# A hybrid decoder step on one Trainium2 core: activations, per-layer input, conv state and norm weights handed over with features as rows, and the first gate and up products taken by turns over the row blocks of x

## The chip, the cores and the metric

The kernel runs on one core of a Trainium2 chip (trn2). The metric is device time in microseconds (us) from launch to end. The engines are PE (TensorE: PE for matmuls, PEld for weight loads), DVE (VectorE), ACT (ScalarE), POOL (GpSimd) and SP (SyncE, which here only issues DMAs). The host arranges the inputs before the launch; what it does is not in the metric.

## The reference, cut to what matters

One layer, for 256 prompt rows and 8 x 4 = 32 sample rows together (288 rows, all float32):

```python
h = h + 0.5 * ((silu(rms(h) @ wg1) * (rms(h) @ wu1)) @ wd1)      # FFN 1: 2048 -> 5632 -> 2048
cb, cc, ch, q, k, v, fl = split(rms(h) @ w_in)                    # 6152 columns
h = h + [rms(cb * conv3(cc * ch)) | rms(forget_attention(q, k, v, fl, paged cache))] @ w_out
h = h + 0.5 * ((silu(rms(h) @ wg2) * (rms(h) @ wu2)) @ wd2)      # FFN 2
h = h + sigmoid(rms(h) @ w_ple_gate) * (p @ w_ple_proj)           # p: 256 features a row
y = rms(h)
```

`rms(x)` scales a row by the inverse root of its mean square and each feature by a norm weight (gain). The convolution carries two earlier rows of each sample sequence (`state_conv`); the sample attention reads 64 pages of cached keys and values by a page table.

## The kernel before, in words

Everything is kept with **features as rows**: `h` is one tile of 128 partitions x 16 blocks x 288 columns, where block k holds features 128k to 128k+127 (a row block, 128 x 288). A product with a weight matrix takes 256 output columns at a time (`pair`, L276 to L308): two banks of PSUM, over all 16 row blocks. float32 is done as float32r in two parts: a value is split in hi and lo, and each 128 x 128 piece of weight takes three matmuls of 288 columns (L298 hi·xh, L299 hi·xl, L300 lo·xh). These are called main matmuls below.

- **Weights** arrive by SP in tiles of 4 row blocks x 256 columns, 512 KB (`load_upto`, L237 to L253), in a ring of `RAW` = 8 buffers: the ninth load waits until the first tile is split. A tile is split in two halves of 2 row blocks (`split_upto`, L257): ACT writes `whi` (L265), DVE `wlo` (L266). There are `HALVES` = 5 buffers for them, so splits run at most five halves ahead of PE. A tile is a **chunk** of 24 main matmuls; a half is 12.
- **x** is made the same way (`split`, L209): ACT `xh` (L210), DVE `xl` (L211), both with the gain column `gT`. The scaling by the inverse root comes later: squares (L226, L229) are added up in `acc` on POOL (L230; the last ones on DVE), PE sums over partitions (L182, L183), DVE and ACT work out the inverse root (L184 to L190), PE spreads it (L206) and DVE copies it into `rs` (L207). `rs` is first used when gate products leave PSUM (`tg`, L358; then ACT `sg` L360, POOL `sr` L362, and `hd`, L367, for up products).
- **The opening**: x comes in as in the reference, rows as rows, in 8 pieces `xa` (128 x 2 x 256) and 8 `xb` (32 x 256). PE turns each row block by three transposes (L412 to L414, in `x_turn`), DVE copies it into `h` (L415), and then it is split and squared. `first` (L432) ties this to the four chunks of the first gate product: turns are placed one chunk ahead, squares behind. The first up product begins when the gate product is through.
- **Gains**: the first norm's are turned by PE at the start (L147), the other seven vectors at step 44 of a written-out list of steps (`later_loads`): 7 loads, 4 more small loads (`bf`, `wf`, `pidx`, `ptb`), then one turn 20 chunks later. From `ptb` DVE works out `idx` (L167), the rows of the paged cache.
- **Keys of the cache**: `k_turn` (from step 50 on) fetches page j + 2 by an indirect DMA of POOL (`kg`, L458) and turns page j on DVE (`kt`, L467), which is written back by four DMAs of POOL (`KD`, L469).
- **Conv state and per-layer input** are loaded as in the reference and turned by PE (L876, 8 transposes; L1078 to L1080, 6).

The order within an engine is not written out: a scheduler places the instructions when the program is built, and each engine then runs its own in that order. `keep_in_program_order` pins some.

Of the kernel before, what the change touches and what calls it, by code (L numbers as in the profile page):

```python
# [25 lines left out]
P = 128  # L26
D = 2048
# [22 lines left out]
TSTEP = 16  # L50

# [37 lines left out]
def build(nc, tc, ctx, A, O):  # L89
# [18 lines left out]
    spare = {"tags": ("kt", "mm"), "at": 0}  # L108
# [22 lines left out]
    def load_gains(names, at, eng):  # L131
        rows = sum(A[n].shape[0] for n in names) // P
        t = W["xs" if at == 0 else "f1"][0].tile([rows, P], F32, name=f"gn{at}", bufs=1)
        r = 0
        for name in names:
            n = A[name].shape[0] // P
            d = eng.dma_start(t[r:r + n, :], A[name].rearrange("(k p) -> k p", p=P))
            if eng is sy:
                tc.keep_in_program_order(d)
            G[name] = at + r  # L140
            r += n
        return t, at

    def turn_gains(t, at):
        b = ktbank()
        r = t.shape[0]
        pe.transpose(b[:, :r], t, ident[:r, :r])  # L147
        v.tensor_copy(gT[:, at:at + r], b[:, :r])
# [75 lines left out]
    def squares(k, work, last_on_v=2):  # L224
        if k == 0:
            s.activation(acc, h[:, k, :], AF.Square)  # L226
        else:
            sq = work.tile([P, NT], F32, name="sq", tag="sq", bufs=2)
            s.activation(sq, h[:, k, :], AF.Square)  # L229
            (v if k >= KT - last_on_v else g).tensor_tensor(acc, acc, sq, ALU.add)  # L230

# [3 lines left out]
    state = dict(loaded=0, split=0, used=0, halves_used=0, chunk=0)  # L235
# [40 lines left out]
    def pair(src, c0, kts, act, evac, k_of=lambda k: k, late=0, tag="mm"):  # L276
# [4 lines left out]
        for ci, ks in enumerate(chunks):  # L281
            it = weight(src, ks[0], len(ks), c0)

            def fn(ci=ci, ks=ks, it=it):
# [3 lines left out]
                split_upto(state["halves_used"] + HALVES)  # L288
# [54 lines left out]
    def ffn(wg, wu, wd, nextgain, work):  # L343
# [3 lines left out]
        for gi, grp in enumerate(groups):  # L347
            def start():
                H["hi"] = work().tile([P, 8, NT], F32R, name="hh", tag="hh", bufs=2)
                H["lo"] = work().tile([P, 8, NT], F32R, name="hl", tag="hl", bufs=2)  # L350
            do(start)
            for pi, pr in enumerate(grp):
# [19 lines left out]
                steps.extend(pair(wg, pr * 256, list(range(KT)), xact, gate, **(dict(late=2, tag="va") if pr == 0 else {})))  # L372
                steps.extend(pair(wu, pr * 256, list(range(KT)), xact, up))
# [25 lines left out]
    def x_load(c):  # L399
        xs = W["xs"][0]  # L400
        cs = slice(c * 256, c * 256 + 256)
        xa = xs.tile([P, 2, 256], F32, name="xa", tag="xa", bufs=8)
        xb = xs.tile([NS, 256], F32, name="xb", tag="xb", bufs=8)
        tc.keep_in_program_order(sy.dma_start(xa, A["x_prompt"][:, cs].rearrange("(j p) c -> p j c", p=P)))
        tc.keep_in_program_order(sy.dma_start(xb, A["x_sample"][:, cs]))
        return xa, xb

    def x_turn(k):
        xa, xb = xin[k // 2]
        w = slice(k % 2 * P, k % 2 * P + P)  # L410
        t = ktbank()
        pe.transpose(t[:, 0:P], xa[:, 0, w], ident)  # L412
        pe.transpose(t[:, P:2 * P], xa[:, 1, w], ident)
        pe.transpose(t[:, 2 * P:NT], xb[:, w], ident[:NS, :NS])  # L414
        v.tensor_copy(h[:, k, :], t[:, :NT])  # L415
        split(X["hi"][:, k, :], X["lo"][:, k, :], h[:, k, :], gain("norm_ffn1", k))
# [6 lines left out]
    opened("xs", "right")  # L423
# [4 lines left out]
    def turns(c):  # L428
        for k in range(4 * c, 4 * c + 4):
            x_turn(k)  # L430

    def first(i, c):  # L432
        run = steps[i][1]

        def fn():
            if c == 0:
                turns(0)
            if c < 3:
                defer(lambda: turns(c + 1), 1)
            if c == 3:  # L440
                spare["tags"] = ("kt",)
                x_squares(3)
                norm_scale(rs, acc, D, 1)
            run()
            if c < 3:
                x_squares(c)
        steps[i] = (steps[i][0], fn)

    for c in range(4):
        first(2 + c, c)  # L450
# [36 lines left out]
    a, b = CONST_COLS["ident"][1:]  # L487
    s.dma_start(C[:, a:b], A["consts"][:, a:b])
    g1 = load_gains(["norm_ffn1"], 0, s)
    for its, _ in steps[2:6]:  # L490
        items.extend(its)
    xin = []
# [378 lines left out]
    def state_in():  # L871
        t = W["fp"][0].tile([16, CB * P], F32, name="stn")
        g.dma_start(t, A["state_conv"])
        b = ktbank()
        for i in range(CB):
            pe.transpose(b[:, 16 * i:16 * i + 16], t[:, i * P:i * P + P], ident[:16, :16])  # L876
# [304 lines left out]
```

## Time and profile before

| | |
|---|---|
| time, 3 runs | median 2389.52 us (2389.41 to 2391.86) |
| the profiled execution's own time | 2396.56 us |
| its span, first to last instruction | 2394.7 us |
| mean granted TensorE clock | 0.995 |
| PE busy | 2365.7 us (99%) |
| DVE, ACT, POOL busy | 60%, 44%, 21% |
| HBM read, written | 469.19 MB, 38.63 MB (212 GB/s over the span) |

How to read the rows that follow: in a window, "34.94 (x196)" is busy time and number of instructions, then come the granted clock, the busy share of the 16 DMA engines and GB/s. In a timeline, a row has start, duration, engine, line, operation, what it writes and reads, and in brackets the idle time before it and what ended that. Matmuls overlap: a row's duration is longer than the distance to the next start, and the distance is what counts. In the waits, a row has the total in us, how many, and the longest.

### The profile page before, as it was taken

The numbers are of one execution on the slowest core, as the hardware profiler recorded it, in microseconds if no ns is written. First come the engines' busy times: TensorE is split into PE (matmuls) and PEld (weight loads), VectorE is DVE, ScalarE is ACT, GpSimd is POOL, SyncE is SP. The second block draws the span as 40 slices with busy tenths as digits, with TensorE's granted clock in tenths as the row PEclk, the third lists the DMA queues.
The fourth block names the chain that finished last, engine by engine and source line by source line (L and its number), as shares of the span: only waits on it lengthen the run. The fifth ranks groups of instructions, "written<-read, shape, count | busy, mean of one in ns | idle before, by whom it ended". The sixth has DMA issues, their size and how long they took to land.

```text
span 2394.7 us, 46026 instructions
## 1 busy us (share of the span) xinstructions
PE 2365.7 (99%) x17856; PEld 2294.7 (96%) x17856; DVE 1430.9 (60%) x2588; ACT 1055.6 (44%) x1858; POOL 498.6 (21%) x688
## 2 busy tenths in 40 slices
PE   8999999999999999999999999999999999999997
PEld 8999999999999999888878899999999999999997
DVE  6556666666655585455456675555555555555765
ACT  5434443444444453333234454444444444444654
POOL 2025354353400011112545310000000000000100
PEclk9999999999999999999999999999999999999998
DMA  7478889898865556987887654545555555555542
GB/s 224 151 247 290 292 281 329 274 310 283 285 227 167 165 166 191 317 306 253 276 292 266 233 167 150 177 153 180 163 165 167 164 163 168 165 161 167 160 158 81
DMA packets 410703, 510.84 MB, mean 213 GB/s; under 512 B 22236, under 2 KB 379316, under 8 KB 406356
## 3 DMA queue, kind: packets, MB, share of 16 engines
q1 hardware_dynamic: 376596, 401.43, 52.4%
q0 software_dynamic: 33664, 106.13, 12.9%
q8 instruction: 140, 2.29, 0.4%
q14 instruction: 79, 0.65, 0.1%
q10 hardware_dynamic: 224, 0.34, 0.1%
HBM read 469.19 MB, written 38.63 MB: 212 GB/s over the span
## 4 chain that ended last, share of the span: by engine, by line
PE 93%; DMA 4%; issue 1%; DVE 1%; POOL 1%; ACT 0%; SPq 0%; POOLq 0%; DVEq 0%; ACTq 0%
PE mm L298 29%; PE mm L300 29%; PE mm L299 28%; DMA page<-in_cache_v_dram,idx 1%; PE va L726 1%; PE va L783 1%; PE va L298 1%; PE va L300 1%; PE va L299 1%; DMA wraw<-in_w_in_dram 1%; DMA bk<-FP 0%; POOL page L250 0%; DMA kg<-in_cache_k_dram,idx 0%; DMA wraw<-in_w_out_dram 0%; DMA xa<-in_x_prompt_dram 0%
## 5 line engine op out<-in xcount | busy, mean ns | idle before, releaser
L266 DVE TENSOR_TENSOR wlo<-wraw,whi 128x512 fp32r<-128x512 f32 x1384 | 967.5, 704 | 737.1 <-ACT whi L265 690.6
L265 ACT ACTIVATE whi<-wraw 128x512 fp32r<-128x512 f32 x1384 | 864.5, 630 | 989.0 <-PE mm L299 915.0
L298 PE MATMUL mm<-xh,whi 128*128 128x288 f32 x3712 | 1109.0, 299 | 0.8 <-DVE tg L358 0.8
L300 PE MATMUL mm<-xh,wlo 128*128 128x288 f32 x3712 | 1093.1, 295 | 3.6 <-DVE wlo L266 3.6
L299 PE MATMUL mm<-xl,whi 128*128 128x288 f32 x3712 | 1096.5, 295 | 0.0
L298 PEld LDWEIGHTS mm<-xh,whi 128*128 128x128 f32 x3712 | 697.1, 188 | 23.3 <-ACT whi L265 14.5
L300 PEld LDWEIGHTS mm<-xh,wlo 128*128 128x128 f32 x3712 | 700.1, 189 | 4.2 <-DVE wlo L266 4.2
L299 PEld LDWEIGHTS mm<-xl,whi 128*128 128x128 f32 x3712 | 698.3, 188 | 0.1
L298 PE MATMUL mm<-hh,whi 128*128 128x288 f32 x1408 | 416.8, 296 | 0.0
L299 PE MATMUL mm<-hl,whi 128*128 128x288 f32 x1408 | 415.4, 295 | 0.0
L300 PE MATMUL mm<-hh,wlo 128*128 128x288 f32 x1408 | 414.0, 294 | 0.0
L362 POOL TENSOR_TENSOR sr<-sg,rs 128x288 f32<-128x288 f32 x88 | 72.8, 828 | 1126.8 <-ACT sg L360 1126.7
L300 PEld LDWEIGHTS mm<-hh,wlo 128*128 128x128 f32 x1408 | 265.1, 188 | 0.0
L299 PEld LDWEIGHTS mm<-hl,whi 128*128 128x128 f32 x1408 | 264.3, 188 | 0.0
L298 PEld LDWEIGHTS mm<-hh,whi 128*128 128x128 f32 x1408 | 263.8, 187 | 0.0
L469 POOL DMA_DIRECT2D KD<-kt x256 | 142.5, 562 | 80.6 <-DVE kt L467 60.6
L230 POOL TENSOR_TENSOR acc<-acc,sq 128x288 f32<-128x288 f32 x66 | 57.1, 865 | 267.1 <-ACT sq L229 222.7
L380 DVE SCALAR_TENSOR_TENSOR h<-mm,h 128x288 f32<-128x288 f32 x192 | 86.7, 453 | 21.3 <-PE mm L300 20.8
L467 DVE STREAM_TRANSPOSE kt<-kg 128x1024 f32<-128x1024 f32 x64 | 79.2, 1238 | 29.0 <-DMA kg<-in_cache_k_dram,idx 22.3
L458 POOL DMA_INDIRECT kg<-in_cache_k_dram,idx x64 | 71.6, 1118 | 74.5 <-DMA wraw<-in_w_ffn_gate_dram 55.5
L360 ACT ACTIVATE sg<-tg 128x288 f32<-128x288 f32 x88 | 39.1, 445 | 104.7 <-DVE tg L358 104.7
L369 ACT ACTIVATE hh<-hd 128x288 fp32r<-128x288 f32 x88 | 39.2, 445 | 96.3 <-DVE hd L367 96.3
(294 smaller groups left out, 1544.0 us busy)
## 6 DMA issues: line engine op xcount, KB each, us to landing
wraw<-in_w_ffn_gate_dram SPq DMA_DIRECT2D x176, 512.0 KB, 3.7
wraw<-in_w_ffn_up_dram SPq DMA_DIRECT2D x176, 512.0 KB, 3.6
wraw<-in_w_ffn_down_dram SPq DMA_DIRECT2D x160, 512.0 KB, 3.6
wraw<-in_w_in_dram SPq DMA_DIRECT2D x96, 512.0 KB, 4.9
KD<-kt POOLq DMA_DIRECT2D x256, 128.0 KB, 5.6
KT<-KD SPq DMA_DIRECT2D x32, 1024.0 KB, 7.3
wraw<-in_w_out_dram SPq DMA_DIRECT2D x32, 512.0 KB, 4.4
wraw<-in_w_ple_gate_dram SPq DMA_DIRECT2D x32, 512.0 KB, 3.6
```

The lines of the kernel that those rows point to most:

```text
L230: (v if k >= KT - last_on_v else g).tensor_tensor(acc, acc, sq, ALU.add)
L265: s.activation(hi, x, AF.Copy)
L266: v.tensor_tensor(lo, x, hi.bitcast(F32), ALU.subtract)
L298: pe.matmul(o, hi[:, j % 2, w], xh, start=f, stop=False)
L299: pe.matmul(o, hi[:, j % 2, w], xl, start=False, stop=False)
L300: pe.matmul(o, lo[:, j % 2, w], xh, start=False, stop=l)
L362: g.tensor_tensor(r, u, rs, ALU.mult)
L369: s.activation(H["hi"][:, k, :], t, AF.Copy)
L380: v.scalar_tensor_tensor(h[:, k, :], o, 0.5, h[:, k, :], ALU.mult, ALU.add)
L458: g.indirect_dma_start(out=KG[j], out_offset=None, in_=A["cache_k"], in_offset=bass.IndirectOffsetOnAxis(ap=idx[:, j:j + 1], axis=0))
L467: v.transpose(t, KG.pop(j).rearrange("p (h d c) -> p d h c", d=4, c=32))
L469: g.dma_start(KD[j // 2, :, j % 2, i].rearrange("(d c) n -> c d n", c=32), t[32 * i:32 * i + 32].rearrange("c d h r -> c d (h r)"))
```

## The change

The host hands over `x` (both groups in one array), `p` and the conv state with features as rows, already in the kernel's 128 x blocks x rows layout (`by_feature`), and all eight vectors of weights as one 128 x 120 array (`gains`). So the 48 transposes of x, the turns of gains (2), conv state (8) and p (6), their copies out of PSUM and their tiles are gone. x is loaded straight into `h` in five loads, `gT` in one on ACT's queue, `consts` in one behind the eighth weight tile.

The chunks of the first gate and the first up product now alternate: gate over row blocks 0 to 3, up over 0 to 3, gate over 4 to 7, and so on. Up uses two `kt` banks of PSUM beside gate's two `va` banks, and both leave PSUM later (`late` 5 and 4). Weight tiles are loaded in the same alternation. The 16 squares run behind chunks 4 to 7, pinned in order, 7 of the adds on POOL and 8 on DVE (before 13 and 2). The sum over partitions is deferred by two chunks after the eighth, its spread by one more. In the list of steps, one step less stands ahead of `later_loads` and of `k_turn` (`closed("xs")` is gone), so both now come one chunk later in the program.

```diff
-    def squares(k, work, last_on_v=2):
+    def squares(k, work, last_on_v=2, pin=False):
...
-                steps.extend(pair(wg, pr * 256, list(range(KT)), xact, gate, **(dict(late=2, tag="va") if pr == 0 else {})))
-                steps.extend(pair(wu, pr * 256, list(range(KT)), xact, up))
+                lead = firstg and pi == 0
+                gs = pair(wg, pr * 256, list(range(KT)), xact, gate, **(dict(late=5 if lead else 2, tag="va") if pr == 0 else {}))
+                us = pair(wu, pr * 256, list(range(KT)), xact, up, **(dict(late=4, tag="kt") if lead else {}))
+                steps.extend([x for gu in zip(gs, us) for x in gu] if lead else gs + us)
...
+    def x_load(a, b):
+        tc.keep_in_program_order(sy.dma_start(h[:, a:b, :], A["x"][:, a:b, :]))
+
+    def x_split(a, b):
+        for k in range(a, b):
+            split(X["hi"][:, k, :], X["lo"][:, k, :], h[:, k, :], gain("norm_ffn1", k))
 
     def x_squares(c):
         for k in range(4 * c, 4 * c + 4):
-            squares(k, W["xs"][0])
+            squares(k, W["f1"][0], 8, True)
...
+    def first(c):
+        run = steps[2 + c][1]
 
         def fn():
             if c == 0:
-                turns(0)
...
+                x_split(0, 2)
+                split_upto(1)
+                x_split(2, 4)
+                state["lead"] = HALVES - 1
+            if c == 1:
+                x_split(4, 8)
+                state["lead"] = HALVES
+            if c in (2, 4):
+                x_split(4 + 2 * c, 8 + 2 * c)
             run()
+            if c >= 4:
+                x_squares(c - 4)
+            if c == 7:
+                norm_scale(rs, acc, D, 2, 1)
...
     def later_loads():
-        t = load_gains(["norm_mix", "norm_ffn2", "norm_ple", "norm_final", "norm_conv_out", "norm_attn_out", "conv_w"], 16, sy)
         small_loads()
-        defer(lambda: turn_gains(*t), 20)
-
-    steps.insert(14, ([], lambda: closed("xs")))
...
+    s.dma_start(gT, A["gains"])
+    for its, _ in steps[2:10]:
         items.extend(its)
     for c in range(4):
-        xin.append(x_load(2 * c))
-        xin.append(x_load(2 * c + 1))
-        load_upto(c + 1)
+        x_load(4 * c, 4 * c + (2 if c == 0 else 4))
+        load_upto(2 * c + 1)
+        if c == 0:
+            x_load(2, 4)
+        load_upto(2 * c + 2)
     items.clear()
-    tc.keep_in_program_order(sy.dma_start(C[:, b:], A["consts"][:, b:]))
-    turn_gains(*g1)
+    tc.keep_in_program_order(sy.dma_start(C, A["consts"]))
...
+        g.dma_start(M["st"].rearrange("p i b t -> p i (b t)"), A["state"])
...
+        g.dma_start(pa, A["p"])
...
+            s.activation(E["hi"][:, k, :], pa[:, k, :], AF.Copy)
+            v.tensor_tensor(E["lo"][:, k, :], pa[:, k, :], E["hi"][:, k, :].bitcast(F32), ALU.subtract)
...
+def by_feature(a):
+
+    return np.ascontiguousarray(a.reshape(a.shape[0], -1, P).transpose(2, 1, 0))
```

The order of the instructions at three places follows. First ACT in the opening, from its first block of x on; before (`xh` is a split block of x, `whi` a split half of weights, `sq` and `acc` squares):

```order
L229 ACTIVATE sq<-h 128x288
L210 ACTIVATE xh<-h,gT 128x288 x3
L265 ACTIVATE whi<-wraw 128x512 x2
L226 ACTIVATE acc<-h 128x288
L210 ACTIVATE xh<-h,gT 128x288
L229 ACTIVATE sq<-h 128x288 x2
L210 ACTIVATE xh<-h,gT 128x288 x2
L265 ACTIVATE whi<-wraw 128x512 x2
```

and now:

```order
L200 ACTIVATE xh<-h,gT 128x288 x2
L257 ACTIVATE whi<-wraw 128x512 x2
L200 ACTIVATE xh<-h,gT 128x288 x2
L257 ACTIVATE whi<-wraw 128x512 x2
L200 ACTIVATE xh<-h,gT 128x288 x4
L257 ACTIVATE whi<-wraw 128x512 x4
L200 ACTIVATE xh<-h,gT 128x288 x4
L257 ACTIVATE whi<-wraw 128x512 x4
L200 ACTIVATE xh<-h,gT 128x288 x4
L257 ACTIVATE whi<-wraw 128x512
L216 ACTIVATE acc<-h 128x288
```

For every four blocks of x there are now four halves of weights where there were two, and no square stands ahead of the last block of x.

Second SP's queue at the later small loads, in the fourth pair of gate and up; before:

```order
L242 DMA wraw<-in_w_ffn_up_dram 128x4x256 x4
L137 DMA gn_1692<-in_norm_mix_dram 16x128
L137 DMA gn_1692<-in_norm_ffn_dram 16x128
L137 DMA gn_1692<-in_norm_ple_dram 16x128
L137 DMA gn_1692<-in_norm_final_dram 16x128
L137 DMA gn_1692<-in_norm_conv_out_dram 8x128
L137 DMA gn_1692<-in_norm_attn_out_dram 8x128
L137 DMA gn_1692<-in_conv_w_dram 24x128
L166 DMA bf<-in_b_f_dram 8x1
L166 DMA wf<-in_w_in_dram 128x16x8
L166 DMA pidx<-in_page_table_dram 64x1
L166 DMA ptb<-in_page_table_dram 128x64
```

and now:

```order
L234 DMA wraw<-in_w_ffn_up_dram 128x4x256 x4
L234 DMA wraw<-in_w_ffn_gate_dram 128x4x256
L156 DMA bf<-in_b_f_dram 8x1
L156 DMA wf<-in_w_in_dram 128x16x8
L156 DMA pidx<-in_page_table_dram 64x1
L156 DMA ptb<-in_page_table_dram 128x64
L234 DMA wraw<-in_w_ffn_gate_dram 128x4x256 x3
```

The seven loads of gains are gone, and the four small loads now stand behind the first gate tile of the fifth pair.

Third DVE behind them (`idx` from `ptb`; `kt` turns a page of keys, `tg` takes a gate product out of PSUM); before:

```order
L167 TENSOR_SCALAR idx<-ptb,consts 128x64
L266 TENSOR_TENSOR wlo<-wraw,whi 128x512 x3
L467 STREAM_TRANSPOSE kt<-kg 128x1024
L266 TENSOR_TENSOR wlo<-wraw,whi 128x512
L467 STREAM_TRANSPOSE kt<-kg 128x1024
L266 TENSOR_TENSOR wlo<-wraw,whi 128x512 x2
L467 STREAM_TRANSPOSE kt<-kg 128x1024
L358 TENSOR_TENSOR tg<-mm,rs 128x288
```

and now:

```order
L157 TENSOR_SCALAR idx<-ptb,consts 128x64
L258 TENSOR_TENSOR wlo<-wraw,whi 128x512 x2
L450 STREAM_TRANSPOSE kt<-kg 128x1024
L258 TENSOR_TENSOR wlo<-wraw,whi 128x512 x2
L450 STREAM_TRANSPOSE kt<-kg 128x1024 x2
L258 TENSOR_TENSOR wlo<-wraw,whi 128x512 x2
L352 TENSOR_TENSOR tg<-mm,rs 128x288 x2
```

`idx` stands behind as many splits as before, but the first page is turned one split earlier, and the third two splits ahead of the first `tg` instead of just ahead of it.

More of the change, by code (lines that the diff above doesn't have):

```diff
@@ L50 @@
 TSTEP = 16
+GAINS = ("norm_ffn1", "norm_mix", "norm_ffn2", "norm_ple", "norm_final", "norm_conv_out", "norm_attn_out", "conv_w")
+A_ROWS = dict(norm_ffn1=D, norm_mix=D, norm_ffn2=D, norm_ple=D, norm_final=D, norm_conv_out=CB * P, norm_attn_out=NH * P,
+              conv_w=3 * CB * P)
 CONST_COLS = {}
@@ L106, in mmbank @@
         return bank("mm", BANKS["mm"])
-    spare = {"tags": ("kt", "mm"), "at": 0}
+    spare = {"tags": ("kt",), "at": 0}
     def ktbank():
@@ L129, in build @@
     G = {}
[L131 to L148, printed above, removed]
+    at = 0
+    for name in GAINS:
+        G[name] = at
+        at += A_ROWS[name] // P
     def gain(name, k):
@@ L222, in make_x @@
         squares(k, work)
-    def squares(k, work, last_on_v=2):
+    def squares(k, work, last_on_v=2, pin=False):
         if k == 0:
-            s.activation(acc, h[:, k, :], AF.Square)
+            i = s.activation(acc, h[:, k, :], AF.Square)
         else:
             sq = work.tile([P, NT], F32, name="sq", tag="sq", bufs=2)
-            s.activation(sq, h[:, k, :], AF.Square)
+            i = s.activation(sq, h[:, k, :], AF.Square)
             (v if k >= KT - last_on_v else g).tensor_tensor(acc, acc, sq, ALU.add)
+        if pin:
+            tc.keep_in_program_order(i)
     steps = []
     items = []
-    state = dict(loaded=0, split=0, used=0, halves_used=0, chunk=0)
+    state = dict(loaded=0, split=0, used=0, halves_used=0, chunk=0, lead=HALVES)
     def load_upto(n):
@@ L287, in fn @@
                 last = ci == len(chunks) - 1
-                split_upto(state["halves_used"] + HALVES)
+                split_upto(state["halves_used"] + state["lead"])
                 state["chunk"] += 1
@@ L347, in ffn @@
         for gi, grp in enumerate(groups):
+            firstg = gi == 0 and nextgain == "norm_mix"
             def start():
@@ L426, in build @@
     do(lambda: closed("f1"))
[L428 to L433, printed above, removed]
+    def first(c):
+        run = steps[2 + c][1]
         def fn():
             if c == 0:
-                turns(0)
[L438 to L443, printed above, removed]
-            run()
[L445 to L450, printed above, removed]
+                x_split(0, 2)
[7 more added lines that the diff above has]
+                x_split(4 + 2 * c, 8 + 2 * c)
+            run()
+            if c >= 4:
+                x_squares(c - 4)
+            if c == 7:
+                norm_scale(rs, acc, D, 2, 1)
+        steps[2 + c] = (steps[2 + c][0], fn)
+    for c in range(8):
+        first(c)
     KD = drp.tile([DB * PAGES // 2, P, 2, 4, NH * 32], F32, name="KD")
@@ L871, in state_in @@
     def state_in():
[L872 to L876, printed above, removed]
         M["st"] = cst.tile([P, CB, DB, 2], F32, name="st")
-        v.tensor_copy(M["st"].rearrange("p i b t -> p (i b t)"), b[:, :CB * 16])
+        g.dma_start(M["st"].rearrange("p i b t -> p i (b t)"), A["state"])
     def conv_pair(i):
@@ L1068, in ple_start @@
         w = W["pl"][0]
-        pa = w.tile([P, 2, PLE], F32, name="pa")
-        pb = w.tile([NS, PLE], F32, name="pb")
-        g.dma_start(pa, A["p_prompt"].rearrange("(j p) c -> p j c", p=P))
-        g.dma_start(pb, A["p_sample"])
+        pa = w.tile([P, 2, NT], F32, name="pa")
+        g.dma_start(pa, A["p"])
         E["hi"] = w.tile([P, 2, NT], F32R, name="ph")
@@ L1171 @@
     host["consts"] = constants()
+    host["x"] = by_feature(np.concatenate([host.pop("x_prompt"), host.pop("x_sample")]))
+    host["p"] = by_feature(np.concatenate([host.pop("p_prompt"), host.pop("p_sample")]))
+    host["state"] = by_feature(host.pop("state_conv"))
+    host["gains"] = np.ascontiguousarray(np.concatenate([host.pop(n) for n in GAINS]).reshape(-1, P).T)
     for name, a in host.items():
```

30 lines of the change are left out of this document (removed).

## Prediction

> **What bounds the kernel now.** I read the page's busy times first:
>
> ```profile
> PE 2365.7 (99%) x17856; PEld 2294.7 (96%) x17856; DVE 1430.9 (60%) x2588; ACT 1055.6 (44%) x1858; POOL 498.6 (21%) x688
> ```
>
> PE is the bound, so the question is where PE does not do main matmuls at full pace. PE by stretches (busy time, instructions, granted clock, DMA share, GB/s) shows two such places:
>
> ```profile
> 0.00:41.00 41.00, 34.94 (x196) 1.00 0.80 251
> 41.00:140.00 99.00, 99.00 (x743) 1.00 0.51 160
> 140.00:165.00 25.00, 20.60 (x125) 0.80 0.76 246
> 165.00:300.00 135.00, 135.00 (x1015) 1.00 0.89 295
> ```
>
> The last row gives the full pace: 135 / 1015 = 0.133 us for one matmul. Of the 196 instructions before 41 us, 48 are turns of x, one turns gains and 12 belong to the inverse root (the next rows), which leaves 135 main matmuls, worth 135 x 0.133 = 18.0 us. By 41.0 us PE is thus **23.0 us behind**. Between 140 and 165 us there is room for 25 / 0.133 = 188 and 125 run: 63 x 0.133 = **8.4 us lost**. Both places are touched. The timeline of PE in the opening, and the work for the inverse root:
>
> ```profile
> 4.56 0.45 PE L412 MATMUL mm<-consts,xa 128*128 128x128 f32 x1 [4.56 <-DMA xa<-in_x_prompt_dram]
> 9.65 0.61 PE L298 MATMUL va<-xh,whi 128*128 128x288 f32 x1
> 20.29 0.52 PE L300 MATMUL va<-xh,wlo 128*128 128x288 f32 x1
> 20.65 0.30 PE L298 MATMUL va<-xh,whi 128*128 128x288 f32 x1
> 34.94 0.61 PE L182 MATMUL kt<-consts,acc 128*128 128x1 f32 x4
> 35.48 0.22 PE L183 MATMUL kt<-consts,acc 128*32 128x1 f32 x2
> 35.63 0.40 PE L300 MATMUL va<-xh,wlo 128*128 128x288 f32 x1
> 40.12 0.97 PE L206 MATMUL kt<-diag,consts 128*128 128x128 f32 x6
> 41.03 0.40 PE L298 MATMUL mm<-xh,whi 128*128 128x288 f32 x1
> ```
>
> The first main matmul starts at 9.65 us, and durations halve only after 20.3 us: until then the array runs at half pace, though the clock column says 1.00. The inverse root takes (35.63 - 34.94) + (41.03 - 40.12) = 1.6 us of PE, and stays.
>
> The second place, on SP, DVE and PE:
>
> ```profile
> 133.00 0.49 SPq L137 DMA_DIRECT2D gn<-in_norm_mix_dram  x1
> 139.21 0.58 SPq L166 DMA_DIRECT2D ptb<-in_page_table_dram  x1
> 139.90 6.89 SPq L242 DMA_DIRECT2D wraw<-in_w_ffn_gate_dram  x4
> 134.26 0.69 DVE L266 TENSOR_TENSOR wlo<-wraw,whi 128x512 fp32r<-128x512 f32 x1
> 144.33 0.26 DVE L167 TENSOR_SCALAR idx<-ptb,consts 128x64 int32<-128x64 int32 x1 [4.58 <-DMA ptb<-in_page_table_dram]
> 144.50 1.89 DVE L266 TENSOR_TENSOR wlo<-wraw,whi 128x512 fp32r<-128x512 f32 x3
> 152.90 1.25 DVE L467 STREAM_TRANSPOSE kt<-kg 128x1024 f32<-128x1024 f32 x1 [6.51 <-DMA kg<-in_cache_k_dram,idx]
> 151.26 0.29 PE L299 MATMUL mm<-xl,whi 128*128 128x288 f32 x1
> 154.78 0.61 PE L300 MATMUL mm<-xh,wlo 128*128 128x288 f32 x1 [3.22 <-DVE wlo L266]
> 159.09 0.61 PE L298 MATMUL mm<-xh,whi 128*128 128x288 f32 x1 [0.77 <-DVE tg L358]
> 163.57 0.44 PE L298 MATMUL mm<-xh,whi 128*128 128x288 f32 x1
> 163.81 0.35 PE L299 MATMUL mm<-xl,whi 128*128 128x288 f32 x1
> ```
>
> DVE stands still for the first page of keys, with splits queued behind it; PE runs dry, and restarts with matmuls 0.24 us apart (163.57 to 163.81). From 159.09, where work is dense again, it takes 4.7 us until full pace returns at 163.81.
>
> **The opening.** The turns go, and up products fill PE beside gate products. I rebuild it from rows. The data rate there, and the prices of the work that feeds PE:
>
> ```profile
> 4.50:7.50 3.00, 2.94 (x12) 1.88 (x13) 0.63 (x2) 0.97 (x2) 0.00 (x0) 1.00 0.88 276
> 7.50:10.00 2.50, 1.12 (x5) 0.70 (x5) 2.38 (x6) 1.89 (x5) 0.00 (x0) 1.00 0.93 308
> L266 DVE TENSOR_TENSOR wlo<-wraw,whi 128x512 fp32r<-128x512 f32 x27 | 19.4, 739 | 7.2 <-ACT whi L265 6.8
> L211 DVE SCALAR_TENSOR_TENSOR xl<-h,gT,xh 128x288 fp32r<-128x288 f32 x16 | 9.8, 650 | 0.0
> L265 ACT ACTIVATE whi<-wraw 128x512 fp32r<-128x512 f32 x27 | 16.1, 623 | 8.9 <-PE mm L299 8.9
> L210 ACT ACTIVATE xh<-h,gT 128x288 fp32r<-128x288 f32 x16 | 8.1, 528 | 5.6 <-DVE h L415 5.1 <-DVE gT L148 0.5
> L229 ACT ACTIVATE sq<-h 128x288 f32<-128x288 f32 x15 | 6.2, 435 | 6.9 <-POOL acc L230 3.7 <-DVE h L415 3.3
> L230 POOL TENSOR_TENSOR acc<-acc,sq 128x288 f32<-128x288 f32 x13 | 13.1, 1008 | 19.6 <-ACT acc L226 10.1 <-ACT sq L229 8.9
> ```
>
> Start: two blocks of x (288 KB) and the gains (60 KB) are about what landed for the first turn at 4.56 (256 KB and the 64 KB identity). The conv state's 64 KB, now fetched at the very start, and the first gate tile of 512 KB follow at 276 GB/s, 2.1 us, so 6.6. One `whi` (0.62) gives the first main matmul at 7.3, one `wlo` (0.74) the first complete triple at 8.0; from there work is dense. Full pace then comes 4.7 us later, at 12.7, taking the row at 159.09. By then 2 + 4.7 / 0.24 = 22 main matmuls are done, worth 2.9 us: PE is 9.8 us behind.
>
> Does it stay fed? Four blocks of x with two tiles are 1.6 MB, 5.2 us at 308 GB/s, and hold 48 main matmuls, 6.4 us: data comes faster than PE uses it, the eighth tile near 24 us, needed near 33. DVE's splits to there are 16 x 0.74 + 16 x 0.65 = 22 us, ACT's 16 x 0.62 + 16 x 0.53 = 18 us, in about 28 us: cover enough. The weak spot is the squares, now bunched behind the last block of x (near 25 us): 7 adds on POOL at 1.0 us that ACT must keep step with (two `sq` buffers), 8 adds on DVE among splits, hence a sum near 39 to 42 us. PE has the sum over partitions behind main matmul 228, which it reaches at 9.8 + 228 x 0.133 = 40.1, and the spread 24 matmuls (3.2 us) later, where the same stretch took 40.12 - 35.48 = 4.6 us with more splits between. So the in-order wait costs 0 to 2.6 us; I take 1.3. Sum: 9.8 + 1.6 + 1.3 = 12.7 behind, against 23.0: **-10.3**. The clock may come 1.7 us earlier or later (0.8 us of time either way), and the wait spans 0 to 2.6: -8.2 to -12.4.
>
> [...]
>
> [...]
>
> **The keys' first pages.** Seven gain loads leave SP's queue, but the small loads now follow one more gate tile, whose buffer is released by the split at 134.26 (done 134.95). They are thus issued from 135.4 instead of 137.2, and `ptb` lands 0.3 to 1.8 us earlier (the lower end if the tile's 512 KB go ahead, 1.6 us): I take 1.1, so the first page is there at 151.8 instead of 152.90 (all on the old time scale). But the page is turned one split earlier: the half whose `wlo` now stands behind it is the second half of the gate product's last chunk, which begins 24 x 0.133 = 3.2 us ahead of the up product's first matmul at 151.1, and its first bank meets that half six matmuls in, at 148.7; so PE stops near 149.0, at the first `wlo` product, and resumes at 151.8 + 1.25 + 0.69 = 153.7: 4.7 us. Then PE has 24 matmuls at 0.24 = 5.8 us of work, and DVE one split, two turns and two splits, 3 x 0.69 + 2 x 1.25 = 4.6 us: the second and third page and `tg` hide behind it, if the pages have landed, and the two later stops go. Half pace for 4.7 us costs 4.7 x (1 - 0.133 / 0.24) = 2.1, and the fourth page, now fetched only behind a `sr` on POOL, perhaps 0.5. Sum 7.3 against 8.4: **-1.1**, between -3.5 and +1.
>
> **Later transposes.** Their price, from the chain and the timeline:
>
> ```profile
> 910.83 0.59 PE kt L876 x8
> 911.43 0.33 PE mm L298
> 2260.83 0.30 PE L300 MATMUL va<-xh,wlo 128*128 128x288 f32 x1
> 2261.73 0.40 PE L298 MATMUL va<-xh,whi 128*128 128x288 f32 x1
> 209.49 0.09 PE kt L147
> ```
>
> Conv state 0.59 + 0.33 - 0.13 = 0.8, p 2261.73 - 2260.83 - 0.13 = 0.8, gains 0.1; PE is dense there, so all of it counts: **-1.7**. The p load was issued long before its use, and that is unchanged.
>
> Sum: -10.3 - 1.1 - 1.7 = **-13.1 us**. The profiled execution's span of 2394.7 would become 2381.6; its own time, 2396.56, lies 7 us above the median of the three runs, 2389.52, and I take the difference from the median: **2376.4 us**.
>
> **The rivals.**
> - *The clock stays low as long as before*, to 20.4 us. For: it did so under turns and short stops, and new stops would do the same. Against: the gate chunk leaves PE no stop. Half pace for 7.7 us more costs 7.7 x 0.44 = 3.4: 2379.8.
> - *The bunched squares hold up ACT and DVE*, and splits come late too: `wlo` was 0.74 on average and 0.69 alone, so POOL's adds slow it. Some 3 us more: 2379.4.
> - *The first page no longer stops PE*, since the DMA queues are emptier with fewer tiles ahead: 7.3 us more, 2369.1. Against: 8.6 us from `idx` (144.33) to the page (152.90), most of it the fetch's own way.
> - *Slower: pages of keys come late all along.* One wait row of before:
>
> ```profile
> DVE kt L467 <- DMA kg<-in_cache_k_dram,idx: 22.3, 10, 6.5
> ```
>
> DVE waited 22.3 us in 10 pages, and PE met only the first few. POOL now issues three pages, not four, before its first `sr`; if the fetches stay one behind, waits past the lead of five halves (5 x 1.6 = 8 us) reach PE, at worst all 22.3: 2376.4 + 22.3 = 2398.7. It decides from the fourth page on.
> - *The opening isn't really shortened*, because x and tiles together are what it waits for: only the later transposes count, 2387.8. Against: by the rates above all of it has landed by 24 us, and before, PE was still at gate products then.
>
> **How the numbers follow.** Forecast 60%, clock 12%, squares 13%, no stop 8%, late pages 4%, no shortening 3%. A measurement of this kernel can tell about 0.2% (4.8 us) from no change; so faster 0.93, same 0.03, slower 0.04. The forecast's own ends are -8.2 + 1 - 1.5 = -8.7 and -12.4 - 3.5 - 1.9 = -17.8. The range reaches over clock and squares, to which some of these errors add, and leaves out the other three (15%): 2371 to 2382.
>
> **What would show it.** Right: no L412 rows; first main matmul near 7.3; full pace near 13; about 12.7 us behind once the spread is done; one stop of 4 to 5 us at the first `kt`, 2 to 3 us earlier in the work than now, and none of 0.77 at `tg`. Wrong: full pace near 20, stops at `whi` or `wlo` before 36 us, a stop of over 3 us at the sum over partitions, or stops at `kt` after the fourth page.

## The result, and the profile after

| | before | after |
|---|---|---|
| median of 5 runs, same chip | 2389.92 us (2389.41 to 2393.01) | 2379.65 us (2373.67 to 2380.13) |
| profiled execution, own time / span | 2396.56 / 2394.7 us | 2380.13 / 2378.2 us |

The ratio of the times, after to before, is 0.9941, with a 95% interval of 0.9928 to 0.9953: by the ratio 14.1 us faster (11.2 to 17.2), by the two medians 10.3. Another set of runs (below) gave 0.9944 (0.9931 to 0.9958), 13.4 us by the ratio and 13.5 by the medians. Between sets, differences of medians move by some us. The two profiled executions lie 16.5 us apart, since that of before was 6.6 us above its median. So the traces tell where time moved; how much it is worth, the timed runs tell.

The busy times on the page of after:

```profile
PE 2350.4 (99%) x17792; PEld 2284.3 (96%) x17792; DVE 1426.0 (60%) x2575; ACT 1052.7 (44%) x1858; POOL 495.6 (21%) x681
```

PE has 64 instructions less and is still the bound. PE by the two stretches that matter, of after (busy, instructions, granted clock, DMA share, GB/s):

```profile
0.00:41.00 41.00, 34.62 (x241) 1.00 0.91 297
130.00:170.00 40.00, 36.36 (x267) 1.00 0.88 295
```

The second one of before, over the same 40 us:

```profile
130.00:170.00 40.00, 35.60 (x238) 0.87 0.73 228
```

Of the 241 instructions before 41 us, 6 belong to the sum over partitions, so 235 main matmuls ran where the kernel before had 135: PE is 41.0 - 235 x 0.133 = 9.7 us behind, 10.6 with the spread (0.9), against 23.0. At the pages, 40 / 0.133 = 301 matmuls have room: 34 are missing after (4.5 us), 63 before (8.4 us). After shows no fall of the clock there, neither in its column (1.00, before 0.87) nor in its matmuls (0.13 us apart behind both of its stops).

The timeline of PE in the opening of after:

```profile
6.38 0.61 PE L290 MATMUL va<-xh,whi 128*128 128x288 f32 x1 [6.38 <-ACT whi L257]
11.60 0.42 PE L292 MATMUL va<-xh,wlo 128*128 128x288 f32 x1
11.84 0.31 PE L290 MATMUL va<-xh,whi 128*128 128x288 f32 x1
39.44 0.50 PE L172 MATMUL kt<-consts,acc 128*128 128x1 f32 x4
40.02 0.40 PE L290 MATMUL mm<-xh,whi 128*128 128x288 f32 x1
43.31 0.94 PE L196 MATMUL kt<-diag,consts 128*128 128x128 f32 x6
44.18 0.40 PE L290 MATMUL mm<-xh,whi 128*128 128x288 f32 x1
```

The main products begin at 6.38 us and not at 9.65; durations fall at 11.84 and not at 20.65; and neither the sum (39.44) nor the spread (43.31) has a wait in brackets. Its squares are early enough. POOL and DVE there:

```profile
24.72 6.93 POOL L220 TENSOR_TENSOR acc<-acc,sq 128x288 f32<-128x288 f32 x7 [22.76 <-ACT sq L219]
```

```profile
32.73 2.15 DVE L220 TENSOR_TENSOR acc<-acc,sq 128x288 f32<-128x288 f32 x4
35.99 2.14 DVE L220 TENSOR_TENSOR acc<-acc,sq 128x288 f32<-128x288 f32 x4
```

The last addition ends at 35.99 + 2.14 = 38.1, 1.3 us before PE asks. The squares do hold up the splits, though: between 24 and 41 us ACT waits 3.6 us for additions of POOL and DVE, and DVE then 3.5 us for a `whi`. The lead of the splits over PE covers this; PE has no stop. The keys' first pages of after, on DVE and then on PE:

```profile
130.35 0.26 DVE L157 TENSOR_SCALAR idx<-ptb,consts 128x64 int32<-128x64 int32 x1 [3.04 <-DMA ptb<-in_page_table_dram]
136.82 1.25 DVE L450 STREAM_TRANSPOSE kt<-kg 128x1024 f32<-128x1024 f32 x1 [5.02 <-DMA kg<-in_cache_k_dram,idx]
139.16 2.37 DVE L450 STREAM_TRANSPOSE kt<-kg 128x1024 f32<-128x1024 f32 x2
152.05 1.25 DVE L450 STREAM_TRANSPOSE kt<-kg 128x1024 f32<-128x1024 f32 x1 [4.09 <-DMA kg<-in_cache_k_dram,idx]
```

```profile
138.70 0.40 PE L292 MATMUL mm<-xh,wlo 128*128 128x288 f32 x1 [1.99 <-DVE wlo L258]
143.13 0.40 PE L290 MATMUL mm<-xh,whi 128*128 128x288 f32 x1 [0.17 <-DVE tg L352]
143.36 0.29 PE L291 MATMUL mm<-xl,whi 128*128 128x288 f32 x1
153.93 0.40 PE L292 MATMUL mm<-xh,wlo 128*128 128x288 f32 x1 [1.47 <-DVE wlo L258]
```

The first page arrives 6.5 us after `idx` (130.35 to 136.82; before, 144.33 to 152.90 was 8.6). PE stops for 2.0 us at the first `wlo` product, runs at full pace behind it (0.29 at 143.36), and stops once more, 1.5 us, at the fourth page.

Further on, three markers of the chain of waits give the balance: the sums over partitions of the second norm, of the one behind the pages of values, and of the last but one. Of before, and of after:

```profile
884.79 0.34 PE kt L182 x4
1289.70 0.34 PE kt L182 x4
2264.39 0.34 PE kt L182 x4
```

```profile
868.31 0.34 PE kt L172 x4
1274.74 0.34 PE kt L172 x4
2247.82 0.34 PE kt L172 x4
```

After is 16.5 us ahead at the first, 15.0 at the second, 16.6 at the third. Between the first two it should have gained 0.8 us more by the conv state; it lost 1.5. The 0.8 us are there: from the first marker to the first matmul with a page of values it takes 259.6 us (868.31 to 1127.9), before 260.4 (884.79 to 1145.2). Some 2.3 us are given back behind that matmul, and nothing in the prediction foresaw it.

### The profile page after: what moved, and what is told of

The parts are those of the page before. It is cut to its first block, busy times and chain, and to the rows that moved or that the text cites. A ratio compares the mean times of both kernels' runs of the same rounds, so it can differ in the third digit from the quotient of the medians.

```text
span 2378.2 us, 45847 instructions
## 1 busy us (share of the span) xinstructions
PE 2350.4 (99%) x17792; PEld 2284.3 (96%) x17792; DVE 1426.0 (60%) x2575; ACT 1052.7 (44%) x1858; POOL 495.6 (21%) x681
## 4 chain that ended last, share of the span: by engine, by line
PE 94%; DMA 3%; issue 1%; DVE 1%; POOL 1%; ACT 0%; SPq 0%; POOLq 0%; DVEq 0%; ACTq 0%
PE mm L290 30%; PE mm L292 29%; PE mm L291 29%; PE va L704 1%; DMA page<-in_cache_v_dram,idx 1%; PE va L761 1%; PE va L290 1%; PE va L292 1%; PE va L291 1%; DMA kg<-in_cache_k_dram,idx 1%; DMA wraw<-in_w_in_dram 1%; DMA wraw<-in_w_out_dram 0%; DVE wlo L258 0%; POOL page L242 0%; PE kt L196 0%
## 5 line engine op out<-in xcount | busy, mean ns | idle before, releaser
L290 PEld LDWEIGHTS mm<-xh,whi 128*128 128x128 f32 x3680 | 690.1, 188 | 22.6 <-ACT whi L257 13.6
L220 POOL TENSOR_TENSOR acc<-acc,sq 128x288 f32<-128x288 f32 x60 | 50.5, 841 | 270.5 <-ACT sq L219 236.7
```

The costliest lines, as they stand in the source:

```text
L290: pe.matmul(o, hi[:, j % 2, w], xh, start=f, stop=False)
```

## The experiments

The theory was the prediction's, with the sizes just read: the opening (about 12 us, part of it the earlier clock), the keys' pages, the later turns. The rivals: that a good part of the gap between the traces is chance; that one piece (the hand-over, the turns by chunk, the clock) does it all.

**The kernel before once more:**

```diff
 MANUAL = False
+AGAIN = True
```

> The kernel before, unchanged, for a second trace: the first one's own time (2396.56 us) lies 6.6 us above the median of the other runs. Theory A (the keys' first pages are what varies): this execution is nearer 2390, the opening is again 23 us behind at 41 us, and the loss at the first pages is 2 to 6 us instead of 8.4, with less time at half pace. Rival (the opening varies, by when the clock comes): the loss at the pages is again about 8 us and the opening is 18 to 20 us behind.

Measured: 2391.77 us, ratio to before 0.9999 (0.999 to 1.0009). Its PE in the two stretches:

```profile
0.00:41.00 41.00, 34.83 (x208) 1.00 0.83 262
130.00:170.00 40.00, 35.75 (x245) 0.91 0.77 237
```

Full pace came at 15.73 us, not 20.65, so 208 - 61 = 147 main matmuls ran by 41 us: 21.4 behind. At the pages 56 are missing, 7.4 us. Neither theory's numbers came: the opening lies between their 23 and 18 to 20, and the loss at the pages above the 2 to 6 of theory A. Both places vary, by 1 to 2 us each, and the first trace of before was the slower one at both.

**Hand-over without the turns by chunk** (gate, then up, as before; squares behind each chunk, 13 of the additions on POOL again):

```diff
-            firstg = gi == 0 and nextgain == "norm_mix"
+            firstg = False
...
-            squares(k, W["f1"][0], 8, True)
+            squares(k, W["f1"][0])
...
-    for c in range(8):
+    for c in range(4):
         first(c)
...
```

> The changed kernel with the hand-over, but gate ahead of up in the first pair as before, squares behind each chunk. Theory A (the turns were the cost; x by features feeds PE densely by itself): full pace comes at 12 to 14 us, PE is 11 to 14 us behind once the spread is done, and the time is 0 to 3 us above the changed kernel. Rival (alternation is what fills PE; gate chunks alone wait for x): stops between chunks, full pace at 17 us or later, 15 to 19 us behind, 4 to 8 us above the changed kernel.

Measured: 2382.42 us, ratio 0.9963 (0.995 to 0.9977), slower than after by 2.8 us at the medians and by about 5 by the ratios. PE's opening:

```profile
0.00:41.00 41.00, 32.69 (x213) 1.00 0.89 290
```

213 - 12 = 201 main matmuls, 14.3 us behind: the turns by chunk are worth 3.7 us of the opening, and the hand-over of x the other 7 to 9. Without the turns by chunk PE had five short stops (0.15 to 0.45 us, 1.6 us in all) for `wlo`, `whi` and `xl` between 20 and 27 us; with them, none. Full pace came at 12.15 us, as theory A had it; the stops are the rival's, and 14.3 lies between its 15 to 19 and the theory's 11 to 14. So the hand-over is the larger part, and the turns by chunk take the stops away.

**Pages fetched early** (small loads at the 28th step, three fetches at the 38th, and the first three turns of pages held at their place):

```diff
...
-    steps.insert(44, ([], later_loads))
...
+    steps.insert(38, ([], lambda: [k_fetch(i) for i in range(3)]))
+    steps.insert(34, ([], lambda: opened("kg", "right")))
+    steps.insert(28, ([], later_loads))
...
```

> The changed kernel with the small loads 16 steps earlier, the first three pages fetched before the pair that turns them, and these three turns pinned in order. Theory A (DVE's wait for the first pages stops PE): no stop at the first three pages, 2.5 to 4.5 us faster than the changed kernel. Rival (the fetches slow weight tiles down, and PE stops for these instead): the stop moves and the time stays within 1.5 us.

Measured: 2378.02 us, ratio 0.9945 (0.9931 to 0.9959). The stop moved. At the pages nothing is lost, but DVE now stands 3.3 us at `idx` for the page table, and PE behind it at 96 us:

```profile
130.00:170.00 40.00, 40.00 (x303) 1.00 0.72 211
```

```profile
94.72 0.25 DVE L157 TENSOR_SCALAR idx<-ptb,consts 128x64 int32<-128x64 int32 x1 [3.34 <-DMA ptb<-in_page_table_dram]
```

```profile
96.00 0.40 PE L290 MATMUL mm<-hh,whi 128*128 128x288 f32 x1 [1.92 <-DVE h L376]
```

Against after, the ratio is no different (0.9945 and 0.9941). As the rival had it, the stop moved and the time stayed; but PE stopped behind the wait for the page table, not for weight tiles, as the rival thought. Between 41 and 130 us 641 matmuls ran, 668 in after: 27 of the 34 matmuls gained at the pages are lost there.

**A busy start** (12 fp32 matmuls of ones on PE, 24 instructions, which add nothing to the result, while the first data is on its way):

```diff
+    busy = diag[:, :P]
+    v.memset(busy, 1.0)
+    wb = mmbank()
+    for _ in range(12):
+        tc.keep_in_program_order(pe.matmul(wb[:, :P], busy, busy, start=True, stop=True))
```

> The changed kernel with 12 matmuls of a constant tile on PE ahead of the first main matmul (about 5 us at half pace). Theory A (the clock is granted by PE's own activity in a window before): full pace at 5 to 9 us instead of 11.8, 1 to 2.4 us faster. Rival (it comes at a set time after the start, or needs main matmuls): full pace again near 11.8 and no gain.

Measured: 2376.34 us, ratio 0.9937 (0.9924 to 0.9951). That is 3.3 us faster than after at the medians, but these are of different sets; the ratios of after, 0.9941 and 0.9944, lie inside the interval, so the timed runs alone don't show the gain. The timeline of PE, which does:

```profile
1.13 5.32 PE L472 MATMUL mm<-diag 128*128 128x128 f32 x24 [1.13 <-DVE diag L469]
6.36 0.40 PE L290 MATMUL va<-xh,whi 128*128 128x288 f32 x1
6.60 0.29 PE L291 MATMUL va<-xl,whi 128*128 128x288 f32 x1
```

Full pace is there from the second main matmul. By 41 us 283 - 30 = 253 main matmuls have run (24 of the others are of ones, 6 the sum's), 18 more than in after, 2.4 us; 5.2 us less of half pace (from 11.84 to 6.60), times the forecast's 0.44, make 2.3. As far as the trace goes, the theory held: matmuls of ones, without the kernel's data, were enough for full pace, which was there 6.60 - 1.13 = 5.5 us after the first of them at the latest. That it is a window before that counts, no run shows.

**The other turns alone.** Of the change, only this, with the loads and copies that go with it; x is still turned:

```diff
...
+    host["p"] = by_feature(np.concatenate([host.pop("p_prompt"), host.pop("p_sample")]))
+    host["state"] = by_feature(host.pop("state_conv"))
+    host["gains"] = np.ascontiguousarray(np.concatenate([host.pop(n) for n in GAINS]).reshape(-1, P).T)
...
```

> The kernel before with gains, conv state and p handed over by feature, and x still turned on TensorE. Theory: the turns of gains, state and p lie on the path, 1.7 us, and the seven gain loads gone from SP's queue bring the page table earlier, worth 0 to 4 us at the keys' first pages; the opening is as before. So 1.7 to 5.7 us faster than before, ratio 0.9976 to 0.9993, with markers after the opening level and 0.8 us gained around each of the two turns. Rival: the later turns are filled up by something else late there, or a page stop that moves gives them back: ratio 0.9995 to 1.0005. If it is more than 6 us faster, the opening was not the main part of the change.

Measured: 2390.96 us, ratio 0.9998 (0.9989 to 1.0007). Its trace has what the theory says: between the markers on both sides of p's turns it takes 846.45 us (1410.62 to 2257.07), 0.86 less than in before (1417.08 to 2264.39), and 28 instead of 56 to 63 matmuls are missing at the pages. But a stop comes behind that window, which neither trace of before has. Its row, and PE in a window that takes it in:

```profile
171.25 0.40 PE L288 MATMUL mm<-xh,whi 128*128 128x288 f32 x1 [1.92 <-DVE hd L357]
130.00:300.00 170.00, 165.61 (x1238) 1.00 0.87 284
```

In front of that `hd` DVE turned a page of keys at 169.61 us, behind a wait of 3.8 us for a write-back (`KD`). Over the longer window before ran 1213 matmuls and 1220, so 18 to 25 more ran here, 2.4 to 3.3 us. The times don't show it: the interval reaches from 2.6 us faster to 1.7 slower, which takes in the 1.7 us of the turns, not the upper part of what was expected. What the gains' loads are worth at the pages stays open; the opening, in any case, is the main part.

**Busy start and early pages.** The matmuls of ones as above, and `idx` parted from its loads:

```diff
...
+    def page_numbers():
+        tc.keep_in_program_order(v.tensor_scalar(idx, ptb, float(P), const("iota"), ALU.mult, ALU.add))
...
-    steps.insert(44, ([], later_loads))
...
+    steps.insert(40, ([], lambda: [k_fetch(i) for i in range(3)]))
+    steps.insert(36, ([], page_numbers))
+    steps.insert(34, ([], lambda: opened("kg", "right")))
+    steps.insert(28, ([], later_loads))
...
```

> The changed kernel with 12 matmuls of ones ahead of its first main matmul (as in the run with the busy start), and with the small loads issued at the 28th step, the page numbers computed at the 36th, three pages of keys fetched at the 40th and the first three turns of pages held at their place. The first try at early pages stopped PE at the page numbers, which waited 3.3 us for the page table; here the loads have eight steps (some 25 us) of lead. Theory: both savings stand side by side, 2.3 us at the start and up to 4.5 us at the pages: 2373 to 2376 us, full pace from 6.6 us, no loss between 60 and 170 us. Rival: what is gained at the keys' pages is given back at the pages of values, where PE arrives earlier than the data: 2376 to 2378.5, with over 5 us of waits for pages there.

Measured: 2374.94 us, ratio 0.9923 (0.991 to 0.9936), the fastest version by median and ratio, though its interval overlaps that of the busy start alone. PE in the two stretches:

```profile
0.00:41.00 41.00, 38.49 (x279) 1.00 0.97 313
130.00:170.00 40.00, 40.00 (x302) 1.00 0.74 221
```

No loss at the pages, none between 41 and 130 us. Both savings stand side by side, as the theory had it: 279 - 30 = 249 main matmuls by 41 us, against 235 in after. The pages of values made PE wait 4.4 us in 6 waits, just under the rival's mark.

**Squares on POOL** (13 of 15 additions there, not 7):

```diff
-            squares(k, W["f1"][0], 8, True)
+            squares(k, W["f1"][0], 2, True)
```

> The changed kernel with 13 of the 15 sums of squares on POOL and 2 on VectorE, instead of 7 and 8: the suspected cost of the bunched squares made larger. Theory: the changed kernel's sum over partitions had no wait because POOL's 7 additions at 1.0 us were done near 32 us; 13 of them end near 38 us, and the last two additions on VectorE near 40, so that TensorE waits 0.5 to 2.5 us at that sum (39.6 us): 2380 to 2382. Rival: the sum has room to spare and VectorE, relieved of six additions, feeds TensorE no worse: 2379 to 2380, no wait at the sum. If TensorE waits over 3 us, the prediction's rival of the bunched squares was closer than the changed kernel's trace let it seem.

Measured: 2379.06 us, ratio 0.9949 (0.9936 to 0.9962). The last two additions, on DVE:

```profile
37.63 1.03 DVE L220 TENSOR_TENSOR acc<-acc,sq 128x288 f32<-128x288 f32 x2 [0.70 <-POOL acc L220]
```

They end at 38.7 us, where the theory had them near 40; PE comes at 40.0 and doesn't wait for the sum. Here the rival was right: the sum has room. That DVE would feed PE no worse was not: beside POOL's additions its two `wlo` from 34.43 us on took 2.50 us together (in after the two from 34.79 on took 1.29), and PE stopped for the first of them, which it doesn't in after:

```profile
35.79 0.40 PE L292 MATMUL mm<-xh,wlo 128*128 128x288 f32 x1 [0.60 <-DVE wlo L258]
```

**The kernel before with a busy start** (the same 12 matmuls).

> The kernel before with the same 12 matmuls of ones ahead of its first turn of x. Theory: the clock is granted on TensorE's own activity, and half pace under main matmuls from 9.65 to between 15.7 and 20.7 us cost the kernel before 2.7 to 4.8 us; with full pace from the first turn this goes, 2 to 5 us faster than before, ratio 0.998 to 0.999. Then about a third of what the change gained in its opening was the earlier clock, and the rest the turns that went. Rival: in the opening of the kernel before TensorE waits for VectorE's copies and splits of x (0.5, 0.53 and 0.65 us a block), so a faster clock only lengthens its waits: under 1 us, ratio 0.9996 to 1.0004, though full pace comes early.

Measured: 2389.70 us, ratio 0.999 (0.9982 to 0.9999), 2.4 us by the ratio. PE's opening:

```profile
0.00:41.00 41.00, 37.94 (x249) 1.00 0.85 265
```

249 - 24 - 61 = 164 main matmuls: 19.2 behind, against 23.0 and 21.4. As expected, at the lower end. With the clock there from the start, the turns still hold PE 19.2 us back, where the changed kernel with the same start is 8.2 back (41 - 253 x 0.133, and 0.9 for the spread): 11 us of the opening are not the clock's.

**The changed kernel once more**, with the same added line, the base of the next.

> The changed kernel once more, unaltered, as the base of the run with a delay and as a second trace. Theory: what the first trace shows as level and place (first main matmul near 6.4, no stop before 60 us, 0.86 us gained between the third norm and the fifth by the turns of p that went) is the kernel's; full pace between 10 and 13.5 us, a loss of 2 to 5 us at the keys' first pages and 405 to 409 us for the stretch with the pages of values (868 to 1275 us) vary from execution to execution. Rival: these are the kernel's as well, and all of them come again within 0.5 us. Either way 2378 to 2381 us.

Measured: 2378.99 us, ratio 0.9944 (0.9931 to 0.9958). First main matmul at 6.26, full pace at 11.24, no stop before 60 us. At the pages:

```profile
130.00:170.00 40.00, 38.50 (x285) 1.00 0.91 308
```

16 matmuls missing, 2.1 us, where the first trace had 4.5; no stop at the fourth page. Level and places are the kernel's, the sizes at the pages vary, as the theory had it.

**With a delay ahead of the pages of values.** The four kernels that turn x take 140 to 144.5 us from the first matmul with a page of values to the next norm, those that don't 147 to 150. Is it that they come there 16 us earlier, before the data? 70 fp32 matmuls of the identity, which add nothing to the result:

```diff
+    def delay():
+        wb = mmbank()
+        for _ in range(70):
+            tc.keep_in_program_order(pe.matmul(wb[:, :P], ident, ident, start=True, stop=True))
+
+    steps.insert(len(steps) - 60, ([], delay))
```

> The changed kernel with 70 fp32 matmuls of the identity (140 instructions at about 0.11 us, 15 us) put into TensorE's order near 680 us, ahead of the stretch with the pages of values. In the traces of the four kernels that still turn x that stretch took 400 to 405 us and was reached at 879 to 885 us; in the six that have x handed over it took 406 to 410 us and was reached at 862 to 871. Theory: the pages of values come at their own time, and TensorE, there earlier, waits for them, so about a third of what is gained ahead is given back: with the delay the stretch is reached near 883, takes 400 to 405 us, and the kernel is 9 to 12 us slower than the changed kernel, not 15. Rival: the stretch's length does not hang on when it is reached (it is the order of instructions there, or chance): it takes 406 to 409 us again, and the kernel is 14 to 16 us slower.

Measured: 2394.52 us, 15.5 slower than the changed kernel; ratio to before 1.0014 (1.0005 to 1.0023). The stretch's two ends, by the tile `page` and by the chain:

```profile
L768 PE MATMUL va<-page,PT x192: 592/592/617, 1141.0 to 1282.1; 128*32 128x512 f32 x192
```

```profile
1288.64 0.34 PE kt L172 x4
```

1288.6 - 1141.0 = 147.6 us, as long as ever. My theory fell: when PE gets there has nothing to do with it.

**The place of the inputs.** The hand-over also takes the unturned x, some 2.4 MB, away from its place ahead of the caches among the inputs. One kernel keeps it there, unread:

```diff
-    host["x"] = by_feature(np.concatenate([host.pop("x_prompt"), host.pop("x_sample")]))
+    host["x"] = by_feature(np.concatenate([host["x_prompt"], host["x_sample"]]))
```

The other is the kernel with the other turns alone, with x behind the weights:

```diff
+    host["x_prompt"] = host.pop("x_prompt")
+    host["x_sample"] = host.pop("x_sample")
```

> The changed kernel with the two unturned inputs of x kept as its first inputs, though nothing reads them, so that the caches of keys and values and all weights stand in the chip's memory at the same distance from the first input as when x is turned. The stretch from the first matmul with a page of values to the next norm took 140 to 144.5 us in the four traces of kernels that turn x and 147 to 149 in those that have it handed over, with the same instructions in the same order on TensorE, and a delay of 15 us ahead of it left it at 147.6. Theory: where the caches lie sets how fast the pages come, so here it takes 140 to 145 us and the kernel 2373 to 2377 us. Rival: the place of the inputs does nothing, and the stretch takes 146.5 to 149 again: 2378 to 2381 us.

Measured: 2379.30 us, ratio 0.9947 (0.9933 to 0.996); the stretch took 1272.4 - 1125.2 = 147.2 us.

> The other way round: the kernel that still turns x, with gains, conv state and p handed over, and the two inputs of x moved behind the weights, so that the caches stand first, as in the changed kernel. Theory (the place of the caches sets how fast pages of values come): the stretch from the first page of values to the next norm, 140.4 us without the move, takes 146 to 149 us, and the kernel is 3 to 7 us slower than without it, 2394 to 2398. Rival: the place does nothing: 140 to 145 us, 2389 to 2392.

Measured: 2391.02 us, ratio 0.9999 (0.9989 to 1.001); the stretch took 1284.3 - 1141.5 = 142.8 us. The rival held both times; the place of the inputs does nothing.

So the stretch is 140.4 to 144.5 us in five traces of kernels that turn x (142.6 on average) and 146.8 to 150.1 in nine of those that don't (147.9). TensorE has the same instructions in the same order there. What I can name is where a part of the time goes, not why. PE's waits for pages of values in that stretch, of after, and then of the kernel with the other turns alone:

```profile
PE va L761 <- DMA page<-in_cache_v_dram,idx: 2.2, 4, 1.1
```

```profile
PE va L770 <- DMA page<-in_cache_v_dram,idx: 0.8, 2, 0.5
```

1.4 us of the 6.4 that lie between these two show as waits for pages. These two are the ends, not the rule: in the first trace of before the waits for pages are 2.2 us too, as in after. Counting every stop of PE in the stretch, whatever it waits for, the five traces have 0.8 to 2.7 us and the nine 3.2 to 5.4, on average 1.9 and 4.2: 2.3 us of the 5.3 between the two families. The rest lies in time in which PE is counted as busy. Neither the time of arrival nor the place of the inputs is the cause; it stays open.

## Why the prediction was right

The forecast was -13.1 us, 2376.4 us in 2371 to 2382, against a median of 2379.65 and, by the ratio, -14.1 us (11.2 to 17.2). The sign and the main term held by the forecast's own mechanism. That the total came so close is in part luck: two errors of 3 to 4 us each, one at the keys' pages and one at the pages of values, stood against one another.

- *The opening*, forecast -10.3: measured -12.4 between the first pair of traces, -11.7 with the repeats of both kernels (22.2 behind on average, then 10.5). First main matmul 6.38 (forecast 7.3), full pace 11.84 (12.7), each a little early, together 0.8 us. No run shows the 1.7 us that the forecast lets the clock come earlier or later; full pace came 0.9 us ahead of 12.7 in after and 1.5 (11.24) in its repeat. The wait at the sum, taken at 1.3 us, was none. The forecast's 9.8 + 1.6 + 1.3 was 9.0 + 1.5 + 0. The squares' rival is out for this kernel: ACT and DVE do wait for the squares, as it says, but PE doesn't; the additions end 1.3 us early, and with 13 of them on POOL PE lost 0.6 us at a split and nothing at the sum. The clock's rival is out too: full pace came 4.0 to 5.7 us after the first main matmul in six traces of kernels with both hand-over and turns by chunk and no busy start, against 6.4 to 11.1 us in the four that turn x without one.
- *The gains' load*, rows of 480 B ahead of the first `xh`, cost nothing that shows: that `xh` started at 4.23 us, and waited last for x.

```profile
4.23 0.96 ACT L200 ACTIVATE xh<-h,gT 128x288 fp32r<-128x288 f32 x2 [1.55 <-DMA h<-in_x_dram]
```

- *The keys' first pages*, forecast -1.1 in -3.5 to +1: -3.9 in the first pair of traces, -4.6 with the repeats, outside its range. The step that failed is the size of the stop, not its place: "so PE stops near 149.0, at the first `wlo` product" is what happened (it stopped at 136.7, which is 149.1 with the opening's 12.4 added), but for 2.0 us and not 4.7. The page came 6.5 us after `idx` and not 8.6, and `idx` itself 0.5 us earlier than forecast. The half pace behind the stop, 2.1 us of the forecast, did not come. The fourth page, forecast 0.5, cost 1.5 once and nothing the next time. So the rival "the first page no longer stops PE" came true in part; the argument against it took the 8.6 us as fixed, and 2 to 3 us of them went. The faster fetch is no chance: from `idx` to the first page it takes 8.4 to 8.6 us in the three traces with the seven loads of gains on SP's queue, and 5.5 to 6.5 in the nine without them that fetch at the same place, x turned or not. How the loads do it isn't shown. How much of it counts in the timed runs is open: the kernel with the other turns alone has 2.4 to 3.3 us of it in its trace, and 0.5 us by its ratio.
- *The later turns*, forecast -1.7: 0.8 at the conv state and 0.86 at p, by the markers. Right. The gains' turn, 0.1 of the forecast, is too small to be read.
- *Not foreseen*: the pages of values, +2.3 us in the first pair of traces, +3.7 with the repeats and +5.3 on average over all traces. The prediction has no term for them. With the pages of keys it about cancels.
- The rival of pages of keys late all along is out: PE has no stop behind the fourth. So is the one that the opening isn't really shortened.

Summed over two traces of each kernel, the terms are -11.7 - 4.6 - 1.7 + 3.7 = -14.3 us; by the ratios, -14.1 and -13.4 were timed, by the medians -10.3 and -13.5. The two profiled executions of before, 2396.56 and 2393.34 us, lie 6.6 and 1.6 us above the medians of their own sets, so a sum made from them has some us too much to win back.

## What to carry to other kernels

Turning data on the matrix engine at the start of a kernel cost time here with the clock and without: with the same busy start PE was 19.2 us behind at 41 us, where the changed kernel, with its turns by chunk, was 8.2 behind; and without one it stayed at half pace until 20.65 and 15.73 us, not until 11.84 and 11.24. Before summing what a start-up edit saves, ask what PE can do in the first microseconds that needs no data: 12 matmuls of ones were worth 2.4 us in the changed kernel's trace, and 2.4 us by the ratio in the kernel before. And take a stall's size from more than one execution: the stop for the first page was 3.2 and 2.3 us in two of before, 2.0 and 1.3 in two of after. Take the window wide enough, too: a stop that has left it may only have moved, as the one at 171 us did.

## What the runs showed of the hardware

- Half pace at the start lasted until 20.65 and 15.73 us in two executions of the same kernel, and until 11.84 and 11.24 in two of the changed one, while the granted clock's column said 1.00 all along. Only durations (0.24 us from matmul to matmul, then 0.13) show it.
- Single stops of PE of 2.0 us (after), 2.2 (x turned, inputs moved) and 2.3 (before once more) left matmuls 0.13 us apart behind them; one of 3.2 us (before) left them 0.24 us apart. So did two shorter ones close together: 2.3 us and then 1.2 (before once more), and 1.9 and then 1.2 (before with a busy start), each with 1.1 us of matmuls between. Stops of 1.1 and 1.4 us as close together did not (the other turns alone). The clock's column from 130 to 170 us agrees: 0.87 (before), 0.91 (before once more) and 0.91 (before with a busy start), against 1.00 (after), 0.99 (x turned, inputs moved) and 1.00 (the other turns alone).
- Behind 5.3 us of matmuls whose operands are all ones, main matmuls came 0.13 us apart from 6.60 us on (the busy start). With no matmul ahead of the main ones, which began at 6.38 us, they did so from 11.84 us on (after).
- The first page of keys landed 8.4 to 8.6 us after its numbers with seven small loads (4 to 12 KB each) on SP's queue some 10 us earlier, and 5.5 to 6.5 us after them without.
- The stretch with the pages of values, the same instructions in the same order on PE, takes 5.3 us longer on average in one family of kernels than in the other, for a reason that neither arrival nor the inputs' place explains.
- DVE's split of 128 x 512 took 0.65 us behind the last of POOL's additions (two in 1.29, after, 34.79 us) and 1.25 beside them (two in 2.50, the squares on POOL, 34.43 us).
